# Delta layer's keys: convolution copies in the scans' PSUM banks, gates stored and broadcast first, loads in pairs, edge copies on ACT

## The chip, the cores and the metric

One core of one Trainium2 chip runs the whole program. The metric is the device time of one execution in microseconds (us); smaller is better. Engines are named as the profile names them: PE is TensorE (PEld its weight loads), DVE is VectorE, ACT is ScalarE, POOL is GpSimd, SP is SyncE, which here only issues DMAs (SPq).

## The reference, cut to what matters

Two layers of a streaming encoder over 1024 frames of width 1024, all in float32. Layer 0 is chunked attention, layer 1 is a gated Delta rule, each followed by a squared-ReLU MLP. The change lies in the Delta layer:

```python
proj = h @ w_in                                   # q, k, v, z and two small columns a, b per head
qkv = silu(causal_conv(qkv, conv_w))              # 4 taps along time, each channel by itself
q, k = l2norm(q) * 128**-0.5, l2norm(k)
beta = sigmoid(b)
g = -exp(a_log) * softplus(a + dt_bias)
gc = cumsum(g)                                    # within each chunk: the "cumulated gates"
decay = exp(gc_i - gc_j)                          # for i >= j, else 0
L = strict_lower((beta k) k^T * decay)            # per head and chunk
u, w = solve(I + L, [beta v, beta k exp(gc)])
# then a scan over chunks, with the state S (128 x 128 per head):
v_new = u_c - w_c S
o_c = (q_c exp(gc)) S + (q k^T * decay)_c v_new
S = S * exp(gc_last) + (k exp(gc_last - gc))^T v_new
```

There are 8 heads of width 128.

## The kernel before, in words

The kernel uses chunks of 128 frames in the Delta layer, so each head has 8. Activations lie with channels on the 128 partitions and time along the row. A projection of one head is 2 halves of 512 frames; each half is 24 matmuls (8 blocks of the inner dimension, three products each, since a float32 weight and input are split into a high and a low part) into one PSUM bank of the ring `acc`. The jobs run k for heads 0 to 7 first, then q and v, then z (`dn_ahead`). For each half, `dn_evac` scales the bank into an SBUF tile `xp` (3 edge columns and 512), and does the convolution: two ACT copies with a per-channel scale (`cy`, `cz`), two DVE operations `scalar_tensor_tensor` that add the other two taps, a POOL addition, and the silu on ACT. In the second half of a head the three edge columns are copied from the first half's tile.

Beside the jobs run tasks. `dn_gates` computes the gates (on 64 partitions, one for each head and chunk) and stores three rows of them to DRAM: the cumulated gates `gc`, the negated `beta` (`nb`), and `exp(gc)` (`eg`). It also stores 64 single numbers, the last of each row of `eg` (`gld`), and loads them back broadcast to all partitions (`gl`), for the scans. `dn_loads` loads a head's row of `gc` broadcast to 128 partitions, into the tiles `row`, `vT`, `qk0` and `qk1` in turn; heads 4 to 7 reuse these, so they wait until the block of the head four before is done (mark `u`). `dn_decays` subtracts, takes the minimum with 0 (8 DVE operations of 128 columns per head) and the exponential (ACT, heads in pairs), and stores the result. `dn_blocks` multiplies k by itself on PE into the two banks of the ring `tp`; DVE multiplies them by the decay into `U`, whose parts are stored; then the mark `u` of that head is set (u0 for head 0, and so on). `dn_solves` (four heads at once) waits for u3 and u7 and works on the two banks `zz`; the scans use small PSUM tiles `s1` and `s2`.

The order of all instructions on PE, DVE, ACT and POOL is written out by a planner while the program is built. It keeps a clock with estimated costs (`Clock`); after each matmul of a job, `turn` resumes those tasks whose turn has come, in order of priority. `until` waits for a mark, `take` for a free buffer of a ring, `sleep` for a given planned time; all three compare with the planned clock, not with the chip. On the chip each engine then runs its list in that order and waits where data are late. The queue of SyncE isn't among the engines whose order is fixed by hand (`ENG`); its DMAs are put in order by the framework.

The lines that the profile names in this part: 1806 loads weights (`wraw`), 1902 the broadcasts (`bcast`), 1990 the three stores of `dn_gates`, 1995 and 1996 `gld` and `gl`, 2207 to 2212 the stores of `U`. Most compute instructions carry line 163, that of a helper which calls the engine; they are told apart by their tiles.

Of the kernel before, what the change touches and what calls it, by code (L numbers as in the profile page):

```python
# [7 lines left out]
F32 = mybir.dt.float32  # L8
F32R = mybir.dt.float32r
I32 = mybir.dt.int32  # L10
AF = mybir.ActivationFunctionType
ALU = mybir.AluOpType
# [4 lines left out]
P = 128  # L17
# [3 lines left out]
HB = 512  # L21
# [13 lines left out]
ATT = (3, 2, 0.5, 1, 1, 0.7, 0.6)  # L35
RINGS = {"pt": 2, "po": 2, "sp": 1, "pr": 6, "bias": 3, "thi": 4, "tlo": 3, "oh": 1, "ot": 2}
ENGINES = {"dn_solves": ("vector",)}
POOLED = ()


def wide(col, p, n):
# [44 lines left out]
TAIL = "0111s2" + "1" * 8 + "2" * 10 + "20" + "1" * 8 + "2" * 8  # L86


G = {'u_first':64,'u_second':1,'u_other':0,'u_last':0, 'm_order': 8, 'load': 2.0, 'dload': 2.0, 'dload0': 2.0, 'att0': 3, 'att1': 2, 'att2': 0.5, 'att3': 1, 'att4': 1, 'att5': 0.7, 'att6': 0.6, 'abias': 5, 'aw': 6, 'arl': 4, 'dn_scans': 0, 'dn_decays': 2, 'dn_blocks': 3, 'dn_solves': 0.5, 'dn_inverses': 2, 'dn_prep_values': 4, 'dn_prep_queries': 5, 'dn_loads': 2, 'dn_outs': 7, 'dw': 8, 'drl': 6, 'dgates': 0.5, 'devac': 1, 'dkeys': 4, 'sl_gates': 5.1, 'sl_load': 3.2, 'sl_solve': 9.0, 'sl_inv': 5.0, 'sl_inv2': 3.0, 'sl_u12': 3.0, 'sl_keys': 2.6, 'sl_bias': 3.0, 'sl_kdup': 2.5, 'sl_front': 0.3, 'sl_split': 0.3, 'sl_out': 0.3, 'sl_od': 2.5, 'sl_arl': 1.0, 'sl_drl': 1.0, 'sl_cols': 2.0, 'c_pe': 0.3, 'c_other': 0.15, 'c_small': 0.12}


class Clock:
# [40 lines left out]
    def spend(self, engine, op, args, more):  # L133
# [3 lines left out]
        elif self.by == "vector" and (self.cost(engine, op, args, more) < 0.3 or op == "tensor_reduce"):  # L137
            start += G["c_small"]
        self.at[engine] = start + self.cost(engine, op, args, more)
# [95 lines left out]
class Trunk:  # L235
# [1465 lines left out]
    def deltanet(self, rhs, finish):  # L1701

        tc = self.tc
        with ExitStack() as es:
            self.tpp = es.enter_context(tc.tile_pool(name="tp", bufs=2, space=PSUM))
            self.sc = es.enter_context(tc.tile_pool(name="sc", bufs=1, space=PSUM))
            self.zz = self.sc.tile([P, 2, HB], F32, name="zz")

            self.dq = es.enter_context(tc.tile_pool(name="dq", bufs=1))
            self.d1 = es.enter_context(tc.tile_pool(name="d1", bufs=1))  # L1710
            self.db = es.enter_context(tc.tile_pool(name="db", bufs=2))
            self.drhs, self.finish = rhs, finish
            self.aux = lambda: self.tpp.tile([P, HB], F32, name=self.nm("tp"), tag="tp")
            rings = {
                "tp": Ring(2, self.aux), "acc": Spare(2, self.bank, self.zz[:, 1]), "nt": Ring(3, self.nt),
                "s1": Spare(1, lambda: self.sc.tile([P, 2, P], F32, name=self.nm("s1"), tag="s1")),
                "s2": Spare(1, lambda: self.sc.tile([P, P], F32, name=self.nm("s2"), tag="s2"))}
            for t, n in (("xp", 2), ("cy", 2), ("cz", 2)):
                rings[t] = Ring(n, lambda t=t, n=n: self.db.tile([P, 64 + HB], F32, name=self.nm(t), tag=t, bufs=n))
            self.begin(rings)  # L1720
            self.silu_at, self.ready_at, self.solved = 0.0, set(), {}
            return self.timed(self.dn_run)
# [181 lines left out]
    def dn_gates(self):  # L1904
        nc, a, rhs = self.nc, self.a, self.drhs
        d1, db = self.d1, self.db
        NQ = 64
# [13 lines left out]
        for n in range(3):  # L1921
            z = d1.tile([P, 8, P], F32, name=f"Zh{n}")
# [12 lines left out]
        def t64(name):  # L1935
            used.append(name)
            return room[(len(used) - 1) // 8][:NQ, (len(used) - 1) % 8]
# [10 lines left out]
        x, y, z, z2, pz, be = t64("gx"), t64("gy"), t64("gz"), t64("gz2"), t64("gp"), t64("be")  # L1948
# [22 lines left out]
        for s in (1, 2, 4, 8, 16, 32, 64):  # L1971
# [3 lines left out]
            if s in (4, 32):  # L1975
                yield
        gc = g0
        eg, ed, bg, ng, nb = t64("eg"), t64("ed"), t64("bg"), t64("ng"), t64("nb")
        nc.scalar.activation(eg, gc, AF.Exp)
        nc.vector.tensor_tensor(ed, gc[:, P - 1 : P].broadcast_to([NQ, P]), gc, ALU.subtract)  # L1980
# [4 lines left out]
        nc.vector.reciprocal(be, be)  # L1985
        nc.vector.tensor_scalar(nb, be, -1.0, None, ALU.mult)

        rows = self.dr.tile([3, NQ, P], F32, name="grows")
        for n, t in enumerate((gc, nb, eg)):
            nc.sync.dma_start(rows[n], t)  # L1990
        self.grows = rows
        self.grow = rows.rearrange("n (h p) t -> n h (p t)", h=8)
        gl = self.gl = d1.tile([P, 8, 8], F32, name="gl")
        gld = self.dr.tile([NQ, 1], F32, name="gld")
        nc.sync.dma_start(gld, eg[:, P - 1 : P])
        nc.sync.dma_start(
            gl.rearrange("p h c -> p (h c)"),
            gld.rearrange("q e -> (q e)").rearrange("(o n) -> o n", o=1).broadcast_to([P, NQ]))
        self.decay = self.dr.tile([8, P, 8, P], F32, name="decay")
        self.mark("rows")  # L2000
        yield
        nc.vector.tensor_tensor(bg, be, eg, ALU.mult)
        yield
# [8 lines left out]
        self.give("tp", tp)  # L2012
        self.mark("cols")
        yield from self.until("u", 0)
        self.add(G["dkeys"], self.dn_prep_keys())

    def dn_ab(self):
# [24 lines left out]
    def dn_loads(self):  # L2042

        yield from self.until("rows")
        for h in range(8):
            if h >= 4:
                yield from self.until("u", h - 4)
            d = self.qks[h % 2].rearrange("p q t -> p (q t)") if h & 2 else self.whole(("row", "vT")[h % 2])
            self.heads["load", h] = d
            self.bcast(d, self.grow[0, h])  # L2050
            yield from self.sleep(G["sl_load"])
            self.mark("load", h)

    def dn_decays(self):

# [47 lines left out]
    def dn_evac(self, c, h, half, ps):  # L2103

        nc = self.nc
        s = slice(half * HB, (half + 1) * HB)
        if c == "z":
            if half == 0:
                if h == 1:
                    yield from self.until("solve", 1)  # L2110
                if h >= 2:
                    yield from self.until("out", h - 2)
                self.heads[c, h] = self.dn_out_of(c, h)
            while (c, h) not in self.heads:
                yield
            t = self.heads[c, h][:, s]
            nc.vector.tensor_tensor(t, ps, self.R[:, s], ALU.mult)
            self.give("acc", ps)
            yield
            nc.scalar.activation(t, t, AF.Silu)  # L2120
        else:
            w = self.convw[:, 8 * "qkv".index(c) + h]
            xp = yield from self.take("xp")
            if half == 0:
                nc.vector.memset(xp[:, 0:3], 0.0)
            else:
                nc.vector.tensor_copy(xp[:, 0:3], self.edge[:, HB : HB + 3])
            self.edge = xp
            nc.vector.tensor_tensor(xp[:, 3 : 3 + HB], ps, self.R[:, s], ALU.mult)
            self.give("acc", ps)  # L2130
            yield
            yt = yield from self.take("cy")
            zt = yield from self.take("cz")
            y, z = yt[:, :HB], zt[:, :HB]
            nc.scalar.activation(y, xp[:, 3 : 3 + HB], AF.Copy, scale=w[:, 3:4])
            nc.scalar.activation(z, xp[:, 1 : 1 + HB], AF.Copy, scale=w[:, 1:2])
            yield
            if c == "k" and h in POOLED:
                nc.gpsimd.tensor_tensor(z, y, z, ALU.add)
                yield  # L2140
                nc.scalar.activation(y, xp[:, 0:HB], AF.Copy, scale=w[:, 0:1])
                nc.vector.scalar_tensor_tensor(z, xp[:, 2 : 2 + HB], w[:, 2:3], z, ALU.mult, ALU.add)
            else:
                nc.vector.scalar_tensor_tensor(y, xp[:, 2 : 2 + HB], w[:, 2:3], y, ALU.mult, ALU.add)
                nc.vector.scalar_tensor_tensor(z, xp[:, 0:HB], w[:, 0:1], z, ALU.mult, ALU.add)
            self.give("xp", xp)
            yield
            nc.gpsimd.tensor_tensor(y, y, z, ALU.add)
            self.give("cz", zt)
            yield  # L2150
            if half == 0:
                for need in self.dn_room(c, h):
                    yield from self.until(*need)
                self.heads[c, h] = self.dn_out_of(c, h)
            while (c, h) not in self.heads:
                yield
            nc.scalar.activation(self.heads[c, h][:, s], y, AF.Silu)
            self.give("cy", yt)
            self.silu_at = self.clock.at["scalar"]
        if half == 1:  # L2160
            self.mark(c, h)
# [321 lines left out]
    def dn_scans(self, odd):  # L2483

        nc, db = self.nc, self.db
        for h in range(odd, 8, 2):
            yield from self.until("values", h)
            vb, WQ, qk, kd, Z = self.heads.pop(h)
            if h:
                yield from self.until(*(("solve", 1) if h == 1 else ("out", h - 2)))  # L2490
            o = self.heads["o", h] = db.tile([P, 8, P], F32, name=self.nm("o"), tag="o")
            st = None
            for p in range(8):
# [12 lines left out]
                s2 = yield from self.take("s2")  # L2506
# [206 lines left out]
```

## Time and profile before

| what | value |
|---|---|
| median of 3 runs | 2500.81 us (2499.35 to 2501.48) |
| the profiled execution | 2498.94 us |
| its span (first to last instruction) | 2496.8 us |
| mean granted TensorE clock | 0.994 |
| PE busy | 2422.3 us, 97% |
| DVE, POOL, ACT busy | 1801.5, 1253.4, 1167.4 us |

The Delta layer's projections begin at about 1205 us of the span; the keys' convolutions run from 1215 to 1334, and the layer's last scans end at about 1757. In a row of the order of time, the first number is the start in us, the second the length, then engine, line, operation, output and inputs; in brackets stands how long the engine was idle before it, and what ended that.

### The profile page before, as it was taken

How to read it: one execution, taken by the hardware profiler on the slowest of the kernel's cores; microseconds unless marked ns; L12 is line 12 of the kernel's file. 1: busy time of each engine (PE TensorE's matmuls, PEld its weight loads, DVE VectorE, ACT ScalarE, POOL GpSimd, SP SyncE). 2: the span in 40 equal slices, each digit the busy share in tenths (PEclk: the TensorE clock that was granted, in tenths of full speed). 3: DMA queues.
4: the chain of work that ended last, by engine and by line, in shares of the span. 5: the costliest groups of instructions: out<-in, count | busy, mean ns of one | idle time of the engine just before them, and what ended most of it. 6: DMA issues, size and time to landing. Idle time of an engine off the chain costs nothing.

```text
span 2496.8 us, 36232 instructions
## 1 busy us (share of the span) xinstructions
PE 2422.3 (97%) x12556; PEld 2015.8 (81%) x12556; DVE 1801.5 (72%) x3176; ACT 1167.4 (47%) x2185; POOL 1253.4 (50%) x1059
## 2 busy tenths in 40 slices
PE   8999999999999999999988999999999999999997
PEld 6888888777788887887777888888787888888886
DVE  6666566678877678888769866555778777688887
ACT  6666666635555533334453443333345555433323
POOL 2444445523666556756434434333416666466655
PEclk9999999999999999999999999999999999999998
DMA  4222222523555887772274222322414555967742
GB/s 162 69 66 68 72 84 92 185 93 118 213 204 212 292 301 239 237 228 93 88 223 152 84 88 82 94 77 77 177 68 185 211 204 214 353 237 243 254 163 85
DMA packets 199928, 398.93 MB, mean 160 GB/s; under 512 B 53232, under 2 KB 67888, under 8 KB 199744
## 3 DMA queue, kind: packets, MB, share of 16 engines
q1 hardware_dynamic: 180016, 351.50, 41.6%
q10 hardware_dynamic: 19728, 45.12, 4.7%
q8 instruction: 99, 1.62, 0.3%
q14 instruction: 85, 0.70, 0.1%
HBM read 257.43 MB, written 130.71 MB: 155 GB/s over the span
## 4 chain that ended last, share of the span: by engine, by line
PE 68%; DVE 7%; DMA 3%; issue 2%; ACT 1%; SPq 0%; POOL 0%; ACTq 0%; DVEq 0%; POOLq 0%
PE y L1040 26%; PE z L1040 12%; PE acc L163 11%; PE acc L1040 7%; PE tp L163 4%; PE acc L306 2%; PE acc L305 2%; PE acc L304 2%; PE zz L163 2%; PE s L163 1%; DVE x L1545 1%; DVE xs L421 0%; DMA wraw<-in_w_up_dram 0%; DVE wlo L1046 0%; DMA gld<-qT 0%
## 5 line engine op out<-in xcount | busy, mean ns | idle before, releaser
L163 PE MATMUL acc<-xs,whi 128*128 128x512 f32 x1728 | 599.9, 410 | 5.2 <-DVE xp L163 2.1
L163 PEld LDWEIGHTS acc<-xs,whi 128*128 128x128 f32 x1728 | 315.8, 190 | 53.8 <-DVE xp L163 1.7
L163 PE MATMUL acc<-xs,wlo 128*128 128x512 f32 x856 | 350.2, 409 | 0.0
L1040 PE MATMUL y<-xs,whi 128*128 128x512 f32 x1008 | 311.6, 390 | 5.2 <-DVE x L1545 1.8
L163 POOL TENSOR_TENSOR wlo<-wraw,whi 128x512 fp32r<-128x512 f32 x126 | 167.0, 1326 | 209.9 <-ACT whi L163 180.5
L1055 POOL TENSOR_TENSOR s<-wraw 128x256 f32<-128x256 f32 (+1 forms) x93 | 91.6, 985 | 356.9 <-DVE a L1046 169.9
L1040 PEld LDWEIGHTS y<-xs,whi 128*128 128x128 f32 x1008 | 188.9, 188 | 47.1 <-DVE x L1545 2.6
L1046 DVE TENSOR_TENSOR wlo<-wraw,whi 128x512 fp32r<-128x512 f32 (+1 forms) x182 | 208.3, 1144 | 25.5 <-ACT whi L1049 25.5
L1049 ACT ACTIVATE whi<-wraw 128x512 fp32r<-128x512 f32 (+2 forms) x191 | 146.4, 767 | 122.6 <-PE y L1040 82.8
L1040 PE MATMUL y<-xs,wlo 128*128 128x512 f32 x504 | 196.3, 389 | 0.0
L1049 ACT ACTIVATE a<-s 128x256 fp32r<-128x256 f32 x122 | 63.8, 524 | 281.6 <-PE y L1040 141.6
L1040 PE MATMUL y<-xs,a 128*128 128x512 f32 x732 | 187.9, 392 | 6.6 <-DVE x L1545 6.6
L1545 DVE TENSOR_TENSOR x<-y,x 128x512 f32<-128x512 f32 x240 | 165.1, 688 | 34.4 <-PE y L1040 26.4
L163 PEld LDWEIGHTS acc<-xs,wlo 128*128 128x128 f32 x856 | 162.9, 190 | 23.4
L1040 PEld LDWEIGHTS y<-xs,a 128*128 128x128 f32 x732 | 135.9, 188 | 40.3 <-DVE x L1545 10.6
L1040 PE MATMUL y<-xs,ahi 128*128 128x512 f32 x512 | 158.6, 391 | 7.8 <-ACT nt L1234 7.8
L1040 PE MATMUL acc<-xs,whi 128*128 128x512 f32 x528 | 162.9, 390 | 0.0
L163 POOL TENSOR_SCALAR pr<-pr,rs 128x640 f32<-128x640 f32 (+4 forms) x128 | 88.1, 691 | 129.4 <-DVE rs L163 98.8
L163 POOL TENSOR_TENSOR cy<-cy,cz 128x512 f32<-128x512 f32 x48 | 62.8, 1309 | 171.2 <-DVE cz L163 117.9
L1040 PE MATMUL z<-xs,whi 128*128 128x512 f32 x480 | 147.8, 389 | 0.0
L1122 DVE TENSOR_TENSOR c<-c 128x512 fp32r<-128x512 f32 x112 | 123.3, 1109 | 30.0 <-POOL c L1052 28.4
L163 DVE CUSTOM_DVE_ANT_0 pr<-sp,bias 128x640 f32<-128x640 f32 (+4 forms) x128 | 83.9, 655 | 63.9 <-PE sp L163 62.9
(367 smaller groups left out, 6060.5 us busy)
## 6 DMA issues: line engine op xcount, KB each, us to landing
xs<-gt SPq DMA_DIRECT2D x256, 256.0 KB, 4.7
gt<-c SPq DMA_DIRECT2D x112, 512.0 KB, 2.9
wraw<-in_w_up_dram SPq DMA_DIRECT2D x64, 512.0 KB, 3.7
wraw<-in_w_down_dram SPq DMA_DIRECT2D x64, 512.0 KB, 4.5
r<-gr SPq DMA_DIRECT2D x88, 256.0 KB, 3.4
wraw<-in_w_in_dram SPq DMA_DIRECT2D x32, 512.0 KB, 3.6
gr<-ssum ACTq DMA_DIRECT2D x62, 256.0 KB, 3.2
wraw<-in_w_qkv_dram SPq DMA_DIRECT2D x30, 512.0 KB, 3.3
```

Source lines behind the costliest of these rows:

```text
L163: return call(*args, **more)
L304: nc.tensor.matmul(ps, hi[:, k], xh, start=(k == 0), stop=False)
L305: nc.tensor.matmul(ps, hi[:, k], xl, start=False, stop=False)
L306: nc.tensor.matmul(ps, lo[:, k], xh, start=False, stop=(k == KT - 1))
L1040: nc.tensor.matmul(ps, w[:, k], x, start=bool(first and f), stop=bool(last and e), skip_group_check=True)
L1046: self.nc.vector.tensor_tensor(lo, src, hi.bitcast(F32), ALU.subtract)
L1049: self.nc.scalar.activation(hi, src, AF.Copy)
L1055: self.nc.gpsimd.tensor_tensor(out, x, y, ALU.add)
L1122: nc.vector.tensor_tensor(t[z][:, HB:].bitcast(F32R), t[z][:, HB:], t[z][:, :HB], ALU.subtract)
L1545: nc.vector.tensor_tensor(x, ps, x, ALU.add)
```

## The change

1. `dn_evac`, keys only: the two ACT copies go to two PSUM banks (rings `py` and `pz`, one buffer each) instead of SBUF; the DVE operations read them there and write `cy` and `cz` in SBUF as before. The two banks are those of the scans' `s1` and `s2`, which become parts of two fixed full-bank tiles; so the scans wait for the last key.
2. `dn_evac`, keys, queries and values: the three edge columns are copied by ACT instead of DVE.
3. `dn_gates`: the store of `gc` and the mark `rows`, on which `dn_loads` waits, come right after the cumulation; the stores of `nb`, `eg` and `gld` come after the later steps, and the load `gl` after u0.
4. `dn_loads`: two heads at a time are loaded; the planned time until the mark `load` is 9.0 us for the first pair and 5.0 for the others, where it was 3.2 for each head.

`POOLED` was empty, so its branch was never taken; it is removed.

```diff
-G = {..., 'sl_load': 3.2, ...}
+G = {..., 'sl_load': 5.0, 'sl_load0': 9.0, ...}
...
+            self.sb = [self.sc.tile([P, HB], F32, name=f"sb{n}") for n in range(2)]
...
-                "s1": Spare(1, lambda: self.sc.tile([P, 2, P], F32, name=self.nm("s1"), tag="s1")),
-                "s2": Spare(1, lambda: self.sc.tile([P, P], F32, name=self.nm("s2"), tag="s2"))}
+                "s1": Spare(1, lambda: self.sb[0][:, : 2 * P].rearrange("p (n t) -> p n t", t=P)),
+                "s2": Spare(1, lambda: self.sb[1][:, :P]),
+                "py": Ring(1, lambda: self.sb[0][:, :]), "pz": Ring(1, lambda: self.sb[1][:, :])}
...
         gc = g0
+        rows = self.grows = self.dr.tile([3, NQ, P], F32, name="grows")
+        self.grow = rows.rearrange("n (h p) t -> n h (p t)", h=8)
+        self.decay = self.dr.tile([8, P, 8, P], F32, name="decay")
+        nc.sync.dma_start(rows[0], gc)
+        self.mark("rows")
...
-        rows = self.dr.tile([3, NQ, P], F32, name="grows")
-        for n, t in enumerate((gc, nb, eg)):
-            nc.sync.dma_start(rows[n], t)
-        self.grows = rows
-        self.grow = rows.rearrange("n (h p) t -> n h (p t)", h=8)
+        nc.sync.dma_start(rows[1], nb)
+        nc.sync.dma_start(rows[2], eg)
         gl = self.gl = d1.tile([P, 8, 8], F32, name="gl")
         gld = self.dr.tile([NQ, 1], F32, name="gld")
         nc.sync.dma_start(gld, eg[:, P - 1 : P])
-        nc.sync.dma_start(
-            gl.rearrange("p h c -> p (h c)"),
-            gld.rearrange("q e -> (q e)").rearrange("(o n) -> o n", o=1).broadcast_to([P, NQ]))
-        self.decay = self.dr.tile([8, P, 8, P], F32, name="decay")
-        self.mark("rows")
...
         yield from self.until("u", 0)
+        nc.sync.dma_start(
+            gl.rearrange("p h c -> p (h c)"),
+            gld.rearrange("q e -> (q e)").rearrange("(o n) -> o n", o=1).broadcast_to([P, NQ]))
         self.add(G["dkeys"], self.dn_prep_keys())
...
-        for h in range(8):
-            if h >= 4:
-                yield from self.until("u", h - 4)
-            d = self.qks[h % 2].rearrange("p q t -> p (q t)") if h & 2 else self.whole(("row", "vT")[h % 2])
-            self.heads["load", h] = d
-            self.bcast(d, self.grow[0, h])
-            yield from self.sleep(G["sl_load"])
-            self.mark("load", h)
+        for g in range(4):
+            for h in range(2 * g, 2 * g + 2):
+                if h >= 4:
+                    yield from self.until("u", h - 4)
+                d = self.qks[h % 2].rearrange("p q t -> p (q t)") if h & 2 else self.whole(("row", "vT")[h % 2])
+                self.heads["load", h] = d
+                self.bcast(d, self.grow[0, h])
+            yield from self.sleep(G["sl_load"] if g else G["sl_load0"])
+            for h in range(2 * g, 2 * g + 2):
+                self.mark("load", h)
...
-                nc.vector.tensor_copy(xp[:, 0:3], self.edge[:, HB : HB + 3])
+                nc.scalar.activation(xp[:, 0:3], self.edge[:, HB : HB + 3], AF.Copy)
...
-            nc.scalar.activation(y, xp[:, 3 : 3 + HB], AF.Copy, scale=w[:, 3:4])
-            nc.scalar.activation(z, xp[:, 1 : 1 + HB], AF.Copy, scale=w[:, 1:2])
+            py, pz = y, z
+            if c == "k":
+                py = yield from self.take("py")
+                pz = yield from self.take("pz")
+            nc.scalar.activation(py, xp[:, 3 : 3 + HB], AF.Copy, scale=w[:, 3:4])
+            nc.scalar.activation(pz, xp[:, 1 : 1 + HB], AF.Copy, scale=w[:, 1:2])
             yield
...
-                nc.vector.scalar_tensor_tensor(y, xp[:, 2 : 2 + HB], w[:, 2:3], y, ALU.mult, ALU.add)
-                nc.vector.scalar_tensor_tensor(z, xp[:, 0:HB], w[:, 0:1], z, ALU.mult, ALU.add)
+            nc.vector.scalar_tensor_tensor(y, xp[:, 2 : 2 + HB], w[:, 2:3], py, ALU.mult, ALU.add)
+            nc.vector.scalar_tensor_tensor(z, xp[:, 0:HB], w[:, 0:1], pz, ALU.mult, ALU.add)
+            if c == "k":
+                self.give("py", py)
+                self.give("pz", pz)
...
             yield from self.until("values", h)
+            yield from self.until("k", 7)
```

More of the change, by code (lines that the diff above doesn't have):

```diff
@@ L37 @@
 ENGINES = {"dn_solves": ("vector",)}
-POOLED = ()
 def wide(col, p, n):
@@ L86 @@
 TAIL = "0111s2" + "1" * 8 + "2" * 10 + "20" + "1" * 8 + "2" * 8
-G = {'u_first':64,'u_second':1,'u_other':0,'u_last':0, 'm_order': 8, 'load': 2.0, 'dload': 2.0, 'dload0': 2.0, 'att0': 3, 'att1': 2, 'att2': 0.5, 'att3': 1, 'att4': 1, 'att5': 0.7, 'att6': 0.6, 'abias': 5, 'aw': 6, 'arl': 4, 'dn_scans': 0, 'dn_decays': 2, 'dn_blocks': 3, 'dn_solves': 0.5, 'dn_inverses': 2, 'dn_prep_values': 4, 'dn_prep_queries': 5, 'dn_loads': 2, 'dn_outs': 7, 'dw': 8, 'drl': 6, 'dgates': 0.5, 'devac': 1, 'dkeys': 4, 'sl_gates': 5.1, 'sl_load': 3.2, 'sl_solve': 9.0, 'sl_inv': 5.0, 'sl_inv2': 3.0, 'sl_u12': 3.0, 'sl_keys': 2.6, 'sl_bias': 3.0, 'sl_kdup': 2.5, 'sl_front': 0.3, 'sl_split': 0.3, 'sl_out': 0.3, 'sl_od': 2.5, 'sl_arl': 1.0, 'sl_drl': 1.0, 'sl_cols': 2.0, 'c_pe': 0.3, 'c_other': 0.15, 'c_small': 0.12}
+G = {'u_first':64,'u_second':1,'u_other':0,'u_last':0, 'm_order': 8, 'load': 2.0, 'dload': 2.0, 'dload0': 2.0, 'att0': 3, 'att1': 2, 'att2': 0.5, 'att3': 1, 'att4': 1, 'att5': 0.7, 'att6': 0.6, 'abias': 5, 'aw': 6, 'arl': 4, 'dn_scans': 0, 'dn_decays': 2, 'dn_blocks': 3, 'dn_solves': 0.5, 'dn_inverses': 2, 'dn_prep_values': 4, 'dn_prep_queries': 5, 'dn_loads': 2, 'dn_outs': 7, 'dw': 8, 'drl': 6, 'dgates': 0.5, 'devac': 1, 'dkeys': 4, 'sl_gates': 5.1, 'sl_load': 5.0, 'sl_load0': 9.0, 'sl_solve': 9.0, 'sl_inv': 5.0, 'sl_inv2': 3.0, 'sl_u12': 3.0, 'sl_keys': 2.6, 'sl_bias': 3.0, 'sl_kdup': 2.5, 'sl_front': 0.3, 'sl_split': 0.3, 'sl_out': 0.3, 'sl_od': 2.5, 'sl_arl': 1.0, 'sl_drl': 1.0, 'sl_cols': 2.0, 'c_pe': 0.3, 'c_other': 0.15, 'c_small': 0.12}
 class Clock:
@@ L2134, in dn_evac @@
             y, z = yt[:, :HB], zt[:, :HB]
-            nc.scalar.activation(y, xp[:, 3 : 3 + HB], AF.Copy, scale=w[:, 3:4])
-            nc.scalar.activation(z, xp[:, 1 : 1 + HB], AF.Copy, scale=w[:, 1:2])
-            yield
[L2138 to L2143, printed above, removed]
-                nc.vector.scalar_tensor_tensor(y, xp[:, 2 : 2 + HB], w[:, 2:3], y, ALU.mult, ALU.add)
-                nc.vector.scalar_tensor_tensor(z, xp[:, 0:HB], w[:, 0:1], z, ALU.mult, ALU.add)
+            py, pz = y, z
[4 more added lines that the diff above has]
+            nc.scalar.activation(pz, xp[:, 1 : 1 + HB], AF.Copy, scale=w[:, 1:2])
+            yield
+            nc.vector.scalar_tensor_tensor(y, xp[:, 2 : 2 + HB], w[:, 2:3], py, ALU.mult, ALU.add)
[3 more added lines that the diff above has]
+                self.give("pz", pz)
             self.give("xp", xp)
```

## Prediction

> **What bounds the kernel now.** I read the page first (the span, and TensorE's share of it), then the work by windows through the Delta layer's first 160 us, then the order of time of TensorE, of VectorE and of the DMA-issuing queue around the place where TensorE stops.
>
> ```profile
> span 2496.8 us, 36232 instructions
> PE 2422.3 (97%) x12556; PEld 2015.8 (81%) x12556; DVE 1801.5 (72%) x3176; ACT 1167.4 (47%) x2185; POOL 1253.4 (50%) x1059
> ```
>
> TensorE is the bound of the whole program, so only time in which it stands still, or runs at a lower granted clock, can be won. Where that is in this layer, the windows say (their first columns: length, then PE, PEld, DVE, ACT and POOL busy, then the granted clock):
>
> ```profile
> 1215.00:1255.00 40.00, 40.00 (x180) 32.80 (x179) 31.47 (x72) 19.70 (x32) 16.86 (x12) 1.00 0.18 63
> 1255.00:1295.00 40.00, 35.06 (x173) 29.72 (x172) 30.39 (x67) 25.68 (x33) 12.94 (x11) 0.91 0.78 244
> 1295.00:1335.00 40.00, 34.71 (x180) 28.25 (x179) 32.96 (x73) 18.01 (x24) 17.64 (x13) 1.00 0.70 216
> 1335.00:1375.00 40.00, 36.57 (x174) 30.29 (x173) 38.94 (x88) 15.82 (x28) 19.15 (x14) 0.96 0.40 121
> ...
> 1265.00:1275.00 10.00, 6.80 (x23) 5.80 (x24) 10.00 (x23) 4.10 (x6) 4.72 (x4) 0.66 0.84 246
> 1365.00:1375.00 10.00, 10.00 (x42) 8.22 (x41) 9.76 (x23) 3.66 (x7) 4.85 (x3) 0.83 0.49 159
> ```
>
> TensorE loses nothing up to 1255, then 4.94, 5.29 and 3.43 us in the next three windows, 13.7 together. The stops in order of time:
>
> ```profile
> 1257.66 0.39 PE L163 MATMUL acc<-xs,wlo 128*128 128x512 f32 x1
> 1258.34 0.39 PE L163 MATMUL acc<-xs,wlo 128*128 128x512 f32 x1
> ...
> 1268.20 2.08 PE L163 MATMUL tp<-k 128*128 128x128 f32 x8 [4.94 <-DVE xp L163]
> 1270.50 0.63 PE L163 MATMUL acc<-xs,wlo 128*128 128x512 f32 x1
> 1271.78 0.63 PE L163 MATMUL acc<-xs,wlo 128*128 128x512 f32 x1
> 1273.40 0.63 PE L163 MATMUL zz<-xs,whi 128*128 128x512 f32 x2
> ...
> 1315.24 1.13 PE L163 MATMUL tp<-k 128*128 128x128 f32 x8 [1.89 <-DVE U L163]
> 1328.03 0.72 PE L163 MATMUL acc<-xs,whi 128*128 128x512 f32 x2 [1.07 <-DVE xp L163]
> 1364.13 1.16 PE L163 MATMUL tp<-qT,WQ 128*128 128x128 f32 x8 [3.43 <-DVE qk L163]
> ```
>
> The largest is 4.94 us before 1268.20. It costs more than its length: three matmuls took 1.28 us after it (1270.50 to 1271.78) against 0.68 before (1257.66 to 1258.34), and this lasts until 1273.40. So 5.2 us ran at 0.68/1.28 of the rate, a loss of 2.4 us more. By the granted clock of the last window the stop at 1364 costs 10 x 0.17 = 1.7 us more in the same way. All in all 13.7 + 2.4 + 1.7 = 17.8 us could be won here.
>
> Why is TensorE late at 1268? It waits for one of the two "tp" banks, which VectorE frees with `U<-tp`. VectorE was late because of loads:
>
> ```profile
> 1253.13 1.66 DVE L163 TENSOR_SCALAR row<-row,gcols 128x128 f32<-128x128 f32 x8 [5.36 <-DMA row<-grows]
> 1257.90 1.66 DVE L163 TENSOR_SCALAR vT<-vT,gcols 128x128 f32<-128x128 f32 x8 [2.49 <-DMA vT<-grows]
> 1264.64 2.90 DVE L163 TENSOR_SCALAR qk<-qk,gcols 128x128 f32<-128x128 f32 x4
> 1267.47 0.68 DVE L163 TENSOR_TENSOR U<-tp,row 128x512 f32<-128x512 f32 x1
> 1301.52 0.88 DVE L163 TENSOR_SCALAR qk<-qk,gcols 128x128 f32<-128x128 f32 x4 [1.90 <-DMA qk<-grows]
> 1312.34 0.88 DVE L163 TENSOR_SCALAR qk<-qk,gcols 128x128 f32<-128x128 f32 x4 [4.33 <-DMA qk<-grows]
> 1264.86 1.37 POOL L163 TENSOR_TENSOR cy<-cy,cz 128x512 f32<-128x512 f32 x1 [1.35 <-DVE cz L163]
> ```
>
> It stood 5.36 us for head 0's broadcast of the cumulated gates and 2.49 us for head 1's, 7.85 in all. The issuing queue shows why they came late, with the time from issue to landing below:
>
> ```profile
> 1238.23 0.48 SPq L1990 DMA_DIRECT2D grows<-kbg  x1
> 1242.97 0.53 SPq L1902 DMA_DIRECT2D row<-grows  x1
> 1250.77 0.33 SPq L1996 DMA_DIRECT2D gl<-gld  x1
> 1251.15 0.43 SPq L1902 DMA_DIRECT2D vT<-grows  x1
> ...
> row<-grows SPq DMA_DIRECT2D x1, 512.0 KB, 10.1
> vT<-grows SPq DMA_DIRECT2D x2, 512.0 KB, 6.1
> grows<-kbg SPq DMA_DIRECT2D x1, 32.0 KB, 1.8
> gld<-qT SPq DMA_DIRECT2D x1, 0.2 KB, 9.1
> ```
>
> The store `gld` (64 single numbers) takes 9.1 us; `gl<-gld` waits for it at the head of the queue until 1250.77, and head 1's load stands behind that. Head 0's load, issued 1242.97, needs 10.1 us, so it ends 2.3 us after `gld` does; that it shares `gld`'s queue is my reading.
>
> **The change, part by part.**
>
> *Gates stored and broadcast first; `gl<-gld` after u0.* The store of the cumulated gates is already issued the moment they exist (1238.23), so that edit by itself gains nothing. What is new is that the pair of loads for heads 0 and 1 may follow it: the store lands at 1240.0, and two loads of 512 KB at the 6.1 us of such loads (median of two) land by about 1247. `gld` and the two other stores come behind them. VectorE then has its data when it runs out of other work (about 1247.8) and gets back up to 7.85 us. That covers the stop of 4.94 with 2.9 to spare, and with the stop goes its slow clock: **-7.3 us** (4.9 + 2.4). The bounds are 0 (loads still behind `gld`) and -7.3. What is late next are heads 2 and 3: asked for 9.0 planned us after the first pair, some 1249, with `gld` still in the way until 1250.8, so they land near 1256; VectorE wants them 7.85 us before 1264.64, at 1256.8. That is tight. `gl` is moved past the first block's stores on the same queue; its first readers are the scans, which follow all the keys and cover it.
>
> *Loads in pairs, 5.0 planned us instead of 3.2.* No instruction is added. Head 4's decay work must now wait for head 5's load, which needs head 1's block (mark u1); but head 4's exponentials are needed only when its keys are ready. The longer planned time lets the planner put other VectorE work where it stood 1.90 and 4.33 us (rows at 1301.52 and 1312.34).
>
> *Copies to PSUM, edge copies by ACT.* The groups of the key phase (1210 to 1336), and one from the outputs further on:
>
> ```profile
> L163 DVE SCALAR_TENSOR_TENSOR cz<-xp,convw,cz 128x512 f32<-128x512 f32 x16 | 13.9, 872 | 0.0
> L163 DVE SCALAR_TENSOR_TENSOR cy<-xp,convw,cy 128x512 f32<-128x512 f32 x16 | 13.4, 837 | 1.7 <-ACT cy L163 1.7
> L163 DVE COPY xp<-xp 128x3 f32<-128x3 f32 x8 | 2.6, 319 | 0.0
> ...
> L163 DVE SCALAR_TENSOR_TENSOR nt<-tp,hnorm,zT x16: 750/751/754, 1476.4 to 1766.5; 128x512 f32<-128x512 f32 x16
> ```
>
> The last row is the same operation with one operand in PSUM: 751 ns and never over 754, though POOL works beside it. The keys' 32 would fall to that: (872 - 751 + 837 - 751) x 16 = 3.3 us of VectorE. The eight edge copies leave VectorE; they are 2.6 us busy, and I count 1.9, as a short copy overlaps its neighbour in part. Together 5.2 us of VectorE. [...]
>
> What VectorE's 5.2 us and the filled waits are worth: the stops from 1295 to 1335 total 5.29 us, all behind VectorE. I take half, **-2.6 us** (bounds 0 and -5.3), since VectorE idles 7.0 us in that window and part of the work only moves into it. The stop at 1364 comes where VectorE is 97% busy with the solve's chain; credited 0 (to -5.1). The sixteen later edge copies, for queries and values, are credited 0: after 1380 TensorE hardly stops.
>
> ACT pays eight small copies in the key phase. No row has ACT copying three columns; between 0.15 (VectorE's) and 0.7 us (a full one) that is 1.2 to 5.7 us, nearer the first, in 120 us where ACT is half idle: 0. ACT writing PSUM isn't in the trace either: between 0.6 us (ACT reading PSUM elsewhere) and 0.7 there is nothing to gain or lose that a half idle engine shows.
>
> *One PSUM bank for each copy instead of two SBUF buffers.* This adds a wait: the next half's copies on ACT must wait until VectorE has read the last half's.
>
> ```profile
> 1241.74 0.71 ACT L163 ACTIVATE cy<-xp,convw 128x512 f32<-128x512 f32 x1
> 1243.49 0.71 ACT L163 ACTIVATE cy<-xp,convw 128x512 f32<-128x512 f32 x1
> 1243.61 0.74 DVE L163 SCALAR_TENSOR_TENSOR cz<-xp,convw,cz 128x512 f32<-128x512 f32 x1
> 1248.88 1.29 POOL L163 TENSOR_TENSOR cy<-cy,cz 128x512 f32<-128x512 f32 x1
> ```
>
> Here the second half's copies began (1243.49) before VectorE had finished the first half's (1243.61 + 0.74). Queued behind the waiting copy on ACT are the next weights' split and the keys' silu. I found three such places among 16; each delays VectorE by up to two copies, 1.3 us, so 0 to 3.9; I take **+1.0**, since VectorE idles about a fifth of 1255 to 1335 and mostly has other work to do.
>
> **Sum**: -7.3 - 2.6 + 1.0 = -8.9 us. The profiled execution took 2498.94 us, its span 2496.8, and the median of the runs is 2500.81, 1.9 above it; the difference is applied to the median: 2491.9 us.
>
> **Rivals.**
>
> *More: all stops go.* -17.8: 2483. For it: every stop named hangs on VectorE being late, and VectorE gains 7.85 + 5.2 us. Against: it is 97% busy until 1375. Chance 0.14.
>
> *No change: the loads come early, but into POOL's busy time.* Four decay steps took 2.90 us at 1264.64 while POOL worked (1264.86), eight took 1.66 at 1253.13 while it did not. From 1243.7 to 1250.2 POOL is busy (last row, 1248.88). If all 16 steps of heads 0 and 1 run at 0.73 instead of 0.21 us, they cost 8.3 us more, and the 7.85 are gone: 2499 to 2502. Loads that still land behind `gld` end there too. Against: POOL's work follows VectorE's, so it falls idle soon. Chance 0.18. [...]
>
> *Slower: ACT and VectorE in lockstep over the single banks.* If VectorE meets the wait of 1.3 us in each of the 16 halves with nothing else to do, that is 21 us; less the 13 it gains, 8 us land on TensorE, with a lower clock behind a stop of over 3 us: 2506 to 2511. It decides from ten halves on (13 us / 1.3). Against: three of 16 now. Chance 0.14.
>
> **How the numbers follow.** The forecast (-5 to -14 us) has 0.54, and the rivals 0.14, 0.18, 0.14. 0.2% is 5 us, about what a measurement can tell from no change. Faster: 0.54 + 0.14 less a little for forecasts that end just inside, 0.66. Same: 0.18 and that little, 0.19. Slower: 0.15. The range runs from below "more" to the top of "no change": 2481 to 2502; alone, the forecast's own is 2487 to 2496.
>
> **What would show it.** Right: `row` and `vT` loads issued by 1243 and landed by 1248; no VectorE wait for them; no stop over 3 us and no lower clock between 1255 and 1275; the keys' operations at 0.75 us; `gl<-gld` issued near u0. Wrong: VectorE waiting for ACT's copies at many halves, ACT idle behind VectorE with the weights' split queued, decay steps at 0.7 us each, or the stop reappearing for heads 2 and 3.

## The result, and the profile after

The changed kernel takes 2483.2 us (median of 6 runs, 2481.2 to 2485.6) against 2500.9 before: a ratio of 0.9929, 95% interval 0.9919 to 0.9940, so 15 to 20 us. (Ratios, here and below, leave disturbed runs out and can differ a little from the quotient of the medians.) The profiled execution has a span of 2482.9 us against 2496.8.

Where it came from, by windows of both kernels. The rows have the same columns as in the prediction; first the changed kernel, with the first window from the layer's start to 1255, then the next 120 us, the middle and the end of the layer:

```profile
1213.60:1255.00 41.40, 41.36 (x188) 34.10 (x189) 32.94 (x71) 22.85 (x40) 15.51 (x12) 1.00 0.26 93
1255.00:1375.00 120.00, 115.46 (x581) 96.72 (x580) 98.81 (x225) 62.07 (x96) 53.64 (x41) 0.99 0.59 186
1375.00:1700.00 325.00, 323.51 (x2524) 274.97 (x2523) 209.87 (x504) 129.92 (x306) 126.10 (x99) 1.00 0.28 85
1700.00:1750.40 50.40, 45.79 (x250) 37.43 (x249) 28.47 (x72) 18.27 (x41) 16.29 (x12) 1.00 0.33 105
```

The kernel before, between the same two events (its layer starts 1.1 us earlier in the span, and reaches the last head's output at 1765.4 instead of 1750.4):

```profile
1212.50:1255.00 42.50, 42.50 (x193) 35.05 (x194) 33.41 (x76) 20.30 (x33) 16.86 (x12) 1.00 0.17 60
1255.00:1375.00 120.00, 106.35 (x524) 88.25 (x523) 102.29 (x226) 59.52 (x84) 49.73 (x37) 0.96 0.63 194
1375.00:1700.00 325.00, 321.92 (x2493) 271.68 (x2492) 205.76 (x504) 126.76 (x287) 123.74 (x97) 0.99 0.27 82
1700.00:1765.40 65.40, 60.78 (x336) 50.12 (x334) 36.95 (x91) 25.09 (x56) 23.76 (x17) 1.00 0.32 103
```

The layer is 552.9 - 536.8 = 16.1 us shorter. (The whole span is only 13.9 shorter: 1.1 us are lost ahead of the layer and 1.1 behind it.) Nine of the 16.1 are TensorE's idle time from 1255 to 1375 (13.65 to 4.54 us), 1.6 its idle time from 1375 to 1700, and 5.4 its busy time: 531.6 to 526.1 for the same matmuls. The granted clock fits that: 0.96 to 0.99 in the 120 us and 0.99 to 1.00 in the next 325. The three largest stops of the prediction's rows (4.94, 3.43 and 1.89 us) are gone; the largest left in those 120 us is 1.81 us, and all that TensorE still idles there, it idles from 1295 to 1335:

```profile
1295.00:1335.00 40.00, 35.46 (x183) 28.98 (x182) 32.89 (x77) 22.09 (x32) 16.01 (x13) 1.00 0.73 238
1335.00:1345.00 10.00, 10.00 (x43) 8.31 (x44) 7.70 (x18) 3.61 (x8) 3.04 (x3) 0.83 0.46 109
...
1334.83 1.58 PE L162 MATMUL tp<-k 128*128 128x128 f32 x8 [1.81 <-DVE U L162]
```

But the data hardly came earlier. The changed kernel's issuing queue, its issue-to-landing times, and VectorE in order of time:

```profile
1239.93 0.49 SPq L1983 DMA_DIRECT2D grows<-kbg  x1
1241.10 0.59 SPq L1999 DMA_DIRECT2D gld<-qT  x1
1242.34 0.35 SPq L1904 DMA_DIRECT2D row<-grows  x1
1242.73 0.43 SPq L1904 DMA_DIRECT2D vT<-grows  x1
```

```profile
row<-grows SPq DMA_DIRECT2D x1, 512.0 KB, 10.5
gld<-qT SPq DMA_DIRECT2D x1, 0.2 KB, 8.3
```

```profile
1252.95 0.88 DVE L162 TENSOR_SCALAR row<-row,gcols 128x128 f32<-128x128 f32 x4 [2.83 <-DMA row<-grows]
1267.81 0.68 DVE L162 TENSOR_TENSOR U<-tp,row 128x512 f32<-128x512 f32 x1
```

`gld` still goes out ahead of the loads, head 0's load still needs 10.5 us, VectorE has it at 1252.95 (before: 1253.13), and the first `U` comes at 1267.81 (before: 1267.47). Counted from the start of the layer, which is 1.1 us later here, that is 1.3 and 0.8 us earlier. Yet TensorE, which stood 4.94 us for that `U`, doesn't stop:

```profile
1262.69 1.05 PE L162 MATMUL tp<-k 128*128 128x128 f32 x8
1267.23 1.05 PE L162 MATMUL tp<-k 128*128 128x128 f32 x8
1269.72 1.05 PE L162 MATMUL tp<-k 128*128 128x128 f32 x8
```

The third of these needs a bank of the two in `tp`, which the first `U` frees. Before, it stood in TensorE's list where TensorE arrived at 1263; here it arrives at 1269.7, with projection matmuls done in between. The list is written by the planner, so I counted, in the lists of all kernels, the projection matmuls ahead of that third product, from the transposition of the norm factors on:

| kernel | matmuls ahead | ratio of time to before |
|---|---|---|
| before | 208 | 1 |
| changed | 232 | 0.9929 |
| loads part alone | 238 | 0.9927 |
| gates part alone | 208 | 0.9987 |
| PSUM part alone | 237 | 0.9959 |
| edge part alone | 234 | 0.9952 |
| planned load time 5.0 alone | 229 | 0.9973 |
| edge copies on ACT, order of before | 208 | 1.0000 |
| half of the PSUM copies, order of before | 208 | 0.9989 |
| changed, loads part undone | 236 | 0.9969 |

At 0.227 us each (0.68 us for three, as shown), 24 more of them are 5.4 us, a little more than the stop. The count tells of this one stop, not of the whole time: gates alone has no stop there with 208, as its data are earlier, and the planned time 5.0 alone, with 229, has others instead (both below).

### The profile page after: what moved, and what is told of

The parts are those of the page before. It is cut to its first block, busy times and chain, and to the rows that moved or that the text cites. A ratio compares the mean times of both kernels' runs of the same rounds, so it can differ in the third digit from the quotient of the medians.

```text
span 2482.9 us, 36204 instructions
## 1 busy us (share of the span) xinstructions
PE 2417.5 (97%) x12556; PEld 2014.5 (81%) x12556; DVE 1789.9 (72%) x3152; ACT 1168.9 (47%) x2209; POOL 1250.5 (50%) x1059
## 4 chain that ended last, share of the span: by engine, by line
PE 70%; DVE 6%; DMA 2%; issue 1%; ACT 1%; POOL 0%; ACTq 0%; DVEq 0%; POOLq 0%; SPq 0%
PE y L1039 26%; PE z L1039 12%; PE acc L162 12%; PE acc L1039 7%; PE tp L162 4%; PE zz L162 2%; PE acc L303 2%; PE acc L305 2%; PE acc L304 2%; PE sb L162 2%; DVE x L1544 1%; DMA wraw<-in_w_up_dram 1%; DVE xs L420 0%; DMA xd<-x 0%; DMA qk<-grows 0%
## 5 line engine op out<-in xcount | busy, mean ns | idle before, releaser
L1045 DVE TENSOR_TENSOR wlo<-wraw,whi 128x512 fp32r<-128x512 f32 (+1 forms) x182 | 209.4, 1151 | 25.6 <-ACT whi L1048 25.6
```

Of the source, the lines that this page charges most:

```text
L1045: self.nc.vector.tensor_tensor(lo, src, hi.bitcast(F32), ALU.subtract)
```

## Each part alone

Theory P: the gain is the order that the planner writes, which now fits the chip, and most of all the planned time of the loads. Theory D: it is VectorE's relief by the PSUM and ACT copies. Theory G (step 1 of the prediction): the early gates.

**Loads alone** (before, with these lines):

```diff
-'sl_load': 3.2,
+'sl_load': 5.0, 'sl_load0': 9.0,
+        for g in range(4):
+            for h in range(2 * g, 2 * g + 2):
...
+            yield from self.sleep(G["sl_load"] if g else G["sl_load0"])
```

> The kernel before with the loads in pairs and their planned times (9.0 and 5.0) alone. Theory P (the planner's times): most of the gain is here, because the planner now expects head 0's and head 1's gates when they really land (1253 in both traces) and no longer has TensorE wait for the first U; 2500.9 -> 2486 to 2491, and no stop of over 3 us at 1268. Theory D (VectorE's relief by PSUM and ACT copies): within 3 us of 2500.9, the stop of 4.94 us stays. Theory G (gates stored first): within 3 us as well.

Measured: 2479.2 us (2476.2 to 2485.9), ratio 0.9927 (0.9910 to 0.9944). P in kind, but 7 us below its range. The loads part alone gives as much as the whole change; the interval contains the whole's. As no operation is added or moved to another engine, it can act only through the orders, those of the four engines and of the DMA queue.

**Gates alone**:

```diff
+        nc.sync.dma_start(rows[0], gc)
+        self.mark("rows")
...
         yield from self.until("u", 0)
+        nc.sync.dma_start(gl..., gld...)
```

> The kernel before with the early store of gc, and the load gl after u0, alone; loads one by one with 3.2 planned us as before. Theory G, and step 1 of the prediction: head 0's load lands by 1248, the stop goes, 2490 to 2494. Theory P: the planner now expects the loads some 4 us earlier still, they land no earlier, TensorE's stop stays or grows: 2500 to 2506. Theory D: within 3 us of 2500.9.

Measured: 2498.2 us, ratio 0.9987 (0.9976 to 0.9998). In the traces the layer's instructions have the order of before on all four engines, and here the load does go out ahead of `gld`:

```profile
1242.25 0.42 SPq L1902 DMA_DIRECT2D row<-grows  x1
1244.47 0.59 SPq L1997 DMA_DIRECT2D gld<-qT  x1
...
1249.49 3.06 DVE L163 TENSOR_SCALAR row<-row,gcols 128x128 f32<-128x128 f32 x8 [0.60 <-DMA row<-grows]
1263.81 0.68 DVE L163 TENSOR_TENSOR U<-tp,row 128x512 f32<-128x512 f32 x1
...
1264.54 1.16 PE L163 MATMUL tp<-k 128*128 128x128 f32 x8
1273.07 1.05 PE L163 MATMUL tp<-k 128*128 128x128 f32 x8
1295.26 1.16 PE L163 MATMUL tp<-k 128*128 128x128 f32 x8 [2.14 <-DVE xp L163]
...
1255.00:1295.00 40.00, 37.03 (x192) 30.52 (x190) 32.62 (x61) 24.22 (x32) 15.57 (x12) 1.00 0.72 221
```

The kernel before, its fourth product and its ninth:

```profile
1279.11 1.05 PE L163 MATMUL tp<-k 128*128 128x128 f32 x8
1298.46 1.16 PE L163 MATMUL tp<-k 128*128 128x128 f32 x8 [0.83 <-DVE xp L163]
```

So early data are real: the first `U` is 3.7 us earlier, the stop before the third product (1264.54) is gone, and so is the slow clock behind it (1.00 in that window instead of 0.91). Counted from the first transposition of the norm factors (1211.87 here, 1210.73 before), the fourth product comes 7.2 us earlier, as step 1 of the prediction priced it. But the waits behind it grew, and at the ninth product, after a stop of 2.14 us, 4.3 are left; the whole program gains 0.13%, 3 us. Head 0's eight decay steps took 3.06 us instead of 1.66: longer, as the rival "into POOL's busy time" had it. G and P both missed: G had the mechanism and the price at the stop, but not the waits behind it, and P had it slower. D's "within 3 us" holds.

**PSUM copies alone, edge copies alone** (the hunks of `dn_evac`, each by itself; the PSUM part with the two fixed banks and the scans' wait for the last key):

```diff
-            nc.scalar.activation(y, xp[:, 3 : 3 + HB], AF.Copy, scale=w[:, 3:4])
+            nc.scalar.activation(py, xp[:, 3 : 3 + HB], AF.Copy, scale=w[:, 3:4])
...
-                nc.vector.tensor_copy(xp[:, 0:3], self.edge[:, HB : HB + 3])
+                nc.scalar.activation(xp[:, 0:3], self.edge[:, HB : HB + 3], AF.Copy)
```

> The kernel before with the keys' convolution copies in the two PSUM banks alone. Theory D: VectorE's 32 operations take 0.74 us in the mean instead of 0.855, and VectorE is ahead: 2490 to 2496. Theory P: the operations get shorter all the same, but the first stop stays, as VectorE still waits for the load: 2496 to 2502. Theory G: no change.

> The kernel before with the 24 edge copies on ACT instead of VectorE alone. Theory D: VectorE loses 9.4 us of busy time over the layer (2.6 in the keys), TensorE's later stops shrink: 2495 to 2499. Theory P: 2498 to 2502, the first stop stays. Theory G: no change.

Measured: 2490.7 us, ratio 0.9959 (0.9942 to 0.9976), and 2487.7 us, ratio 0.9952 (0.9937 to 0.9967). At first sight D, and more than it expected of the edge copies. But the counts above say that both also have new orders, so relief and order are mixed here; the runs with the old order, below, part them.

## Each part taken away

The changed kernel with one part undone.

> The changed kernel with its loads one by one and 3.2 planned us again. Theory P: TensorE stops again behind the first U, most of the gain is lost: 2493 to 2500, a stop of 4 us or more around 1265 to 1270. Theory D: the gain stays, 2483 to 2487.

> The changed kernel with the stores of the gates in the old order and the load gl in its old place. Theory G: the gain is lost, 2492 to 2500. Theory P: head 0's and 1's loads land as late as before, and are planned as late or later: 2481 to 2489.

> The changed kernel with the keys' convolution copies in SBUF again. Theory D: 5 us or more of the gain are lost, 2488 to 2496. Theory P: 2483 to 2488, for VectorE's 3.7 us are partly covered.

> The changed kernel with the edge copies on VectorE again. Theory D: 2 to 6 us of the gain are lost, 2485 to 2490. Theory P: 2483 to 2486.

| undone | us | ratio to before | 95% interval |
|---|---|---|---|
| loads | 2493.0 | 0.9969 | 0.9958 to 0.9980 |
| gates | 2484.1 | 0.9934 | 0.9918 to 0.9951 |
| PSUM | 2484.3 | 0.9937 | 0.9922 to 0.9952 |
| edge | 2481.3 | 0.9925 | 0.9910 to 0.9940 |

Only the loads are missed: the other three intervals contain 0.9929. (The edge copies undone came out below both ranges.) What the loads part does is seen in VectorE's waits for broadcasts (the view of who waited for whom, VectorE alone, 1210 to 1340; the columns are us in total, times, and the longest). The kernel before, 17.1 us together:

```profile
DVE qk L163 <- DMA qk<-grows: 6.2, 2, 4.3
DVE vT L163 <- DMA vT<-grows: 5.5, 2, 3.0
DVE row L163 <- DMA row<-grows: 5.4, 1, 5.4
```

The changed kernel, 4.1:

```profile
DVE row L162 <- DMA row<-grows: 2.8, 1, 2.8
DVE qk L162 <- DMA qk<-grows: 1.3, 1, 1.3
```

The changed kernel without the loads part, 24.2, with the stop of TensorE that comes of it:

```profile
DVE qk L162 <- DMA qk<-grows: 10.1, 2, 6.2
DVE row L162 <- DMA row<-grows: 7.8, 2, 5.4
DVE vT L162 <- DMA vT<-grows: 6.3, 1, 6.3
...
1313.56 0.88 DVE L162 TENSOR_SCALAR qk<-qk,gcols 128x128 f32<-128x128 f32 x4 [6.16 <-DMA qk<-grows]
1318.99 1.19 PE L162 MATMUL acc<-xs,whi 128*128 128x512 f32 x2 [10.27 <-DVE frt L162]
```

The stop is not where theory P had it, at 1265 to 1270 (the third product has 236 matmuls ahead of it), but 50 us later: TensorE waits for an `acc` bank, and the scaling that empties it stands on VectorE behind the decay steps of 1313.56. A load planned to land after 3.2 us takes 5.7 to 10.5 in the rows shown. The planner then puts the decay steps at the head of VectorE's list, and everything behind them waits with them.

## The same order, with and without the relief

**Edge copies on ACT, the planner told otherwise.** All lists keep the order of before; only the 24 copies change engines.

```diff
-                nc.vector.tensor_copy(xp[:, 0:3], self.edge[:, HB : HB + 3])
+                self.clock.spend("vector", "tensor_copy", (xp[:, 0:3],), {})
+                self.nc.real.scalar.activation(xp[:, 0:3], self.edge[:, HB : HB + 3], AF.Copy)
```

> The kernel before with the 24 edge copies on ACT, but the planner is told that VectorE does them, so that everything else keeps the order of before. Moved alone with the planner's knowledge they brought 13 us. If that was VectorE's relief, it comes again: 2485 to 2490. If it was the new order that the planner wrote (theory P in its wider form), the gain is small: 2495 to 2500, and the stop of about 5 us at 1268 stays.

Measured: 2501.5 us, ratio 1.0000 (0.9989 to 1.0011): not even the small gain of the second range. In the traces the orders are those of before. VectorE is relieved, and TensorE stops all the same, 3.79 us here:

```profile
L2128 ACT ACTIVATE xp<-xp 128x3 f32<-128x3 f32 x8 | 1.5, 189 | 1.8 <-DVE cz L163 1.8
...
1270.13 2.07 PE L163 MATMUL tp<-k 128*128 128x128 f32 x8 [3.79 <-DVE xp L163]
```

**Half of the PSUM copies, the planner knowing nothing.** One copy of each key half goes to PSUM, the two halves into two banks. (The two fixed banks and the scans' wait for the last key come with it; in the traces the orders are those of before.)

```diff
+            py = self.sb[half][:, :] if c == "k" else y
-            nc.scalar.activation(y, xp[:, 3 : 3 + HB], AF.Copy, scale=w[:, 3:4])
+            nc.scalar.activation(py, xp[:, 3 : 3 + HB], AF.Copy, scale=w[:, 3:4])
```

> The kernel before with one of the two convolution copies of each key half in PSUM (the first half's in one bank, the second half's in the other, so that none waits for the half before), the planner knowing nothing of it: the order of before. Relief of half the size: if relief made the 10 us of the PSUM part, about half of it, 2494 to 2497. If the order did, 2498 to 2502, though VectorE's cy operations take 0.74 us.

Measured: 2499.5 us, ratio 0.9989 (0.9978 to 1.0001). The operations did get shorter (736 ns in the mean, 837 before), and little came of it:

```profile
L163 DVE SCALAR_TENSOR_TENSOR cy<-xp,convw,sb 128x512 f32<-128x512 f32 x16 | 11.8, 736 | 1.6 <-ACT sb L163 1.6
...
1267.50 1.53 PE L163 MATMUL tp<-k 128*128 128x128 f32 x8 [3.69 <-DVE xp L163]
```

For the edge copies this settles it: what they gave alone was the order's. For PSUM it excludes that half the relief is half of 10 us; the other half wasn't tried by itself.

**The planned time alone**: one number.

```diff
-'sl_load': 3.2,
+'sl_load': 5.0,
```

> The kernel before with one number changed: the planned time of each load is 5.0 us instead of 3.2; loads one by one, no pairs, same stores. Theory P: the planner puts the first decays later, TensorE's matmuls that need them too, and the stop of 4.94 us goes or shrinks below 2: 2482 to 2493. If the pairs or the 9.0 us are what counts: 2496 to 2502.

Measured: 2495.1 us, ratio 0.9973 (0.9962 to 0.9985): faster, at less than half the gain of the loads part. The stop at 1268 went, as the third product now has 229 matmuls ahead of it, but two others came:

```profile
1290.10 2.08 PE L163 MATMUL tp<-k 128*128 128x128 f32 x8 [6.04 <-DVE U L163]
1318.74 1.19 PE L163 MATMUL acc<-xs,whi 128*128 128x512 f32 x2 [4.12 <-DVE frt L163]
```

My range missed the time by 2 us. The 9.0 for the first pair, the pairs, or both are needed for the rest; which of them stays open. It also stays open whether the good order comes of truer numbers, or is one good order among others: the PSUM and the edge part alone say nothing of loads, and wrote orders that pass the first stop, too (237 and 234). A planned time that is too long was not tried.

**Really early data, with the good order**: the loads part alone, and `gld` moved behind u0.

```diff
-        nc.sync.dma_start(gld, eg[:, P - 1 : P])
         yield from self.until("u", 0)
+        nc.sync.dma_start(gld, eg[:, P - 1 : P])
+        nc.sync.dma_start(gl..., gld...)
```

> The loads part alone (as in the run of 2479 us) and the store gld moved behind u0 as well, so that nothing slow stands ahead of the first loads. Head 0's and head 1's loads should land by 1248. Step 1 of the prediction (early data are worth time): 2 to 5 us below that run, 2474 to 2477. Theory P: the planner does not know, so nothing is done earlier on TensorE: 2477 to 2481.

Measured: 2480.9 us, ratio 0.9914 (0.9890 to 0.9938). Head 0's load now lands 5.7 us after its issue instead of 9.0 in the loads part alone, and nobody is faster for it, as VectorE's list has the decay steps later anyway. The first `U` comes 25.6 us after the store of `gc` was issued (1238.59 here, 1236.91 there) in both; the last row is that of the loads part alone:

```profile
row<-grows SPq DMA_DIRECT2D x1, 512.0 KB, 5.7
...
1264.14 0.69 DVE L163 TENSOR_TENSOR U<-tp,row 128x512 f32<-128x512 f32 x1
...
1262.49 0.69 DVE L163 TENSOR_TENSOR U<-tp,row 128x512 f32<-128x512 f32 x1
```

The loads alone, with or without this, and the whole change can't be told apart by these runs.

## Why the prediction was right or wrong

The direction, the range and the place were right: most of the gain came from TensorE's stops between 1255 and 1375 and the clock behind them. But that the time fell inside the range is in part luck, for the step with most of the sum did not happen. The forecast of -8.9 us was half of the -17.7 measured. That is the number of the rival "all stops go" (-17.8), but not its mechanism, which had VectorE 13 us ahead (7.85 and 5.2). By windows of 40 us from 1255, TensorE's idle time went from 4.94, 5.29 and 3.43 us to 0, 4.54 and 0.

- *Step 1, early gates and loads, -7.3.* The stop and its slow clock went (1.00 from 1265 to 1275, 0.66 before), but not by this. The loads landed at about the old time, behind `gld`, and so did the first `U`. "Loads still behind `gld`" was my bound of 0 for the step; it happened, and the gain came from the order. Where the load did go out first (gates alone), the stop and its slow clock went as priced, 7.2 us, but later waits, which the step had not counted, had taken 3 of them by the ninth product, and the program kept 3. My reading that head 0's load is held up by `gld` fits the times from issue to landing: 10.1 us before, 10.5 in the changed kernel and 9.0 in the loads part alone, all with `gld` issued 1.2 to 1.3 us ahead of it; 7.1 in gates alone, where `gld` went out 2.2 us behind it, and 5.7 with `gld` behind u0. Why it takes longer behind `gld` is not shown.
- *Loads in pairs and 5.0 planned us.* I gave them a paragraph and no term of their own; the waits that they fill shared the -2.6. They were the part that carried the change: 0.9927 alone, and the only part that is missed when it is taken away. The failure is one of method: I priced the planned times as a wait, and not as the thing that orders TensorE's list.
- *VectorE's relief, -2.6.* The stops that it was to halve hardly shrank (5.29 to 4.54 from 1295 to 1335). The durations came out as said (738 and 739 ns for 751, below, beside medians of 744 and 742 in the same phase of the kernel before; the edge copies left VectorE), but the worth did not: with the order held, the edge copies gave 0.0% and half of the PSUM copies 0.1%, an interval that reaches 0.

```profile
L162 DVE SCALAR_TENSOR_TENSOR cy<-xp,convw,sb 128x512 f32<-128x512 f32 x16 | 11.8, 739 | 4.0 <-ACT sb L162 3.2 <-POOL cy L162 0.8
L162 DVE SCALAR_TENSOR_TENSOR cz<-xp,convw,sb 128x512 f32<-128x512 f32 x16 | 11.8, 738 | 0.0
L162 ACT ACTIVATE xp<-xp 128x3 f32<-128x3 f32 x10 | 1.9, 188 | 0.0
```

- *The single banks, +1.0.* VectorE waited 3.2 us for ACT's copies in all (first row), inside my 0 to 3.9. The longer of its two waits, 2.39 us, ended at 1264.66, and TensorE, busy from 1255 to 1295 without a break, did not feel it. The lockstep rival didn't come.
- *The stop at 1364, 0.* It went too, 3.43 us. The slow clock behind it went as well, but one of the same size stands behind the stop of 1.81 us now (0.83 from 1335 to 1345), so the granted clock of 1335 to 1375 is 0.96 in both kernels. From 1335 to 1375 the changed kernel's VectorE is busy 35.30 us where it was 38.94.
- *After 1375, 0.* The rest of the layer gained 3.6 us: 1.6 of idle time and some 2 of the 5.4 busy time (by windows of 10 us, the slow clock up to 1375 cost 5.1 us before and 1.7 now, which is 3.4 of the 5.4). With the stop at 1364, this is what I set too low.
- *The rival "into POOL's busy time"* happened for head 0 in the gates-alone kernel, by the length of its steps (3.06 us for eight), and did not eat the gain; in the changed kernel half of head 0's steps ran beside POOL: four took 3.11 us at 1255.06, with POOL busy from 1255.22 to 1257.88, and the other four 0.88 us at 1252.95, with POOL idle. No run shows what makes them longer there.
- *The clock.* The rival "slower" has a lower clock "behind a stop of over 3 us". In the changed kernel it came behind one of 1.81 (0.83 from 1335 to 1345).

## What to carry to other kernels

Where a planner with a clock of its own writes the order, a number in that clock is part of the program: compare it with the landing time in the trace, before relieving any engine, and look at the order that comes out of a new one. Here it gave 0.7% with the pairs and 0.3% without; that a truer number gives a better order elsewhere is not shown. Price a change in such a kernel by two questions, what the engines do faster and what order comes out, and part them by a run that makes the engine change behind the planner's back. Gains of parts measured alone don't add here: 18, 12, 10 and 3 us alone by their ratios, 18 together.

## What the runs showed of the hardware

In the changed kernel ACT wrote PSUM a little faster than SBUF: the same copy of 128x512 took 675 ns (median) into PSUM for the keys and 714 into SBUF for the queries and values.

```profile
L162 ACT ACTIVATE sb<-xp,convw x32: 670/675/695, 1216.8 to 1314.9; 128x512 f32<-128x512 f32 x32
L162 ACT ACTIVATE cy<-xp,convw x32: 705/714/726, 1319.8 to 1694.2; 128x512 f32<-128x512 f32 x32
```

Head 0's load of 512 KB landed 9.0 us after its issue in the loads part alone, where the store of 64 single numbers was issued ahead of it on the same queue, and 5.7 us after it with `gld` moved back, 3.3 us less.

The granted clock differed between two executions with the same order on three engines: 0.50 and 1.00 in the rows below. The run with `gld` behind u0 has the order of the loads part alone on TensorE, VectorE and ACT; its profiled execution had half the clock for a while behind a stop of 1.05 us (1383.39), the other (second row) the full clock:

```profile
1385.00:1395.00 10.00, 10.00 (x72) 7.62 (x71) 3.64 (x10) 2.39 (x5) 1.90 (x2) 0.50 0.22 54
1385.00:1395.00 10.00, 9.82 (x86) 7.79 (x85) 8.45 (x20) 2.35 (x5) 2.98 (x4) 1.00 0.33 87
```
